# Channel mixers' output projections: 8 of 22 contraction tiles by 7 block products, weight sums by accumulating DMAs

## The chip, the cores and the metric

The kernel runs on one core of a Trainium2 chip. The metric is the device time of one execution, in microseconds; the median of the runs of a kernel is compared with that of the other. Engines are named as in the profile: PE multiplies matrices (PEld loads its stationary operand), DVE and ACT work on tiles elementwise, POOL is the general engine, SP issues DMAs. A bank is one of eight accumulators of 128 x 512 float32 that PE writes.

## The reference, cut to what matters

Two layers, each a token mixer and then a channel mixer, over 512 tokens of width 1024. The change concerns the last product of the channel mixer (2816 = 22 x 128 hidden channels) and the residual behind it.

```python
def conv_ffn(x, w_in, conv_w, conv_b, w_out):
    h = causal_dwconv(x @ w_in, conv_w, conv_b)
    g, u = jnp.split(h, 2, axis=-1)
    return (jax.nn.silu(g) * u) @ w_out
...
        f = conv_ffn(x, ffn_w_in[i], ffn_conv_w[i], ffn_conv_b[i], ffn_w_out[i])
        x = layer_norm(DN_ALPHA * x + f, ln_g[i, 1], ln_b[i, 1])
```

## The kernel before, in words

Every float32 operand is split in two: `hi` is the value rounded to float32r (a cast on ACT), `lo` the rest (a subtraction on DVE). A product is then three matmuls, hi by hi, hi by lo and lo by hi, each 128 x 128 by 128 x 512.

**Weights.** All weights lie in one list `wall` of tiles of 128 x 1024 (512 KB). `w_prep` loads them in list order on SP's queue into `wraw` (3 buffers) and splits them into `whi` and `wlo` (7 buffers each). `w_get(i)` keeps the preparation 6 tiles ahead of use.

**Channel mixer (`ffn`).** The input projection takes 44 weight tiles; each is 8 contraction steps x 3 = 24 matmuls into one bank (`InProj.get`, `mm_k`, lines 126 to 128, moving operands `xT_hi` and `xT_lo`). ACT and DVE apply the convolution and the gate and write `h`, 22 tiles of 128 channels x 512 tokens. The output projection (`out_proj`) then holds all eight banks (`acc`, 4 token tiles x 2 halves of the width) and goes through the 22 contraction tiles: for each, `split.get(k)` splits tile k of `h` into `ahi` and `alo` (6 buffers, lines 192 and 193), and 24 matmuls (lines 214 to 216) add its product to the eight banks. `stats` reads the banks with the residual `xres` (line 259) for the normalisation.

**Order.** The program is built with a tile framework that places instructions on each engine's queue by its own estimate of when they can run; each engine then works strictly through its queue, waiting on semaphores. So what stands ahead of what in a queue is fixed before the run.

Of the kernel before, what the change touches and what calls it, by code (L numbers as in the profile page):

```python
# [47 lines left out]
HEAD = 96  # L48
WB = 7
LOOK = 6  # L50


@with_exitstack
def trunk_kernel(ctx, tc, x_tok, x_t, w_dt, wall, pp, ln_g, ln_b, b_v, b_s, w_s_t, out):
# [15 lines left out]

    wready = {}
    wnext = [0]

    def w_prep(upto):
        while wnext[0] <= min(upto, W_ALL - 1):
            i = wnext[0]
            raw = wpool.tile([P, 1024], F32, tag="wraw", bufs=3, name=f"wraw{i}")
            nc.sync.dma_start(raw, wall[i])
            hi = wpool.tile([P, 1024], F32R, tag="whi", bufs=WB, name=f"whi{i}")
            nc.scalar.copy(hi, raw)  # L80
            lo = wpool.tile([P, 1024], F32R, tag="wlo", bufs=WB, name=f"wlo{i}")
# [41 lines left out]
    def mm_k(o, w, k, lo, hi):  # L123
        whi, wlo = w
        cs = slice(k * P, (k + 1) * P)
        nc.tensor.matmul(o, whi[:, cs], xT_hi[:, k, lo:hi], start=(k == 0), stop=False)  # L126
        nc.tensor.matmul(o, whi[:, cs], xT_lo[:, k, lo:hi], start=False, stop=False)  # L127
        nc.tensor.matmul(o, wlo[:, cs], xT_hi[:, k, lo:hi], start=False, stop=(k == NK - 1))  # L128

    with tc.tile_pool(name="xload", bufs=8) as xl:  # L130
        wdt = xl.tile([P, NK, 32], F32, name="wdt", bufs=1)
        xr = []
        for q in range(4):
            for k in (2 * q, 2 * q + 1):
# [48 lines left out]
    class Split:  # L183
# [3 lines left out]

        def pre(self, k, tag=""):
            bufs = self.bufs if not tag else 1
            hi = self.pl.tile([P, T], F32R, tag="ahi" + tag, bufs=bufs, name=f"ahi{self.base}_{k}")  # L190
            lo = self.pl.tile([P, T], F32R, tag="alo" + tag, bufs=bufs, name=f"alo{self.base}_{k}")
            nc.scalar.copy(hi, self.act(k))  # L192
            nc.vector.tensor_sub(lo, self.act(k), hi.bitcast(F32))  # L193
            self.done[k] = (hi, lo)

        def get(self, k):
# [8 lines left out]
    def out_proj(lnp, split, base, nk, ln, last, hooks=None, nxt=None, mid=None):  # L205
        if last:
            gb, bb = ln_bc(lnp, base, ln)
        acc = [[pst(f"acc{base}_{t}_{h}") for h in range(2)] for t in range(NT)]

        def mm(t, h, k, a, w):  # L210
            o = acc[t][h]
            ts_ = slice(t * P, (t + 1) * P)
            hs = slice(h * T, (h + 1) * T)
            nc.tensor.matmul(o, a[0][:, ts_], w[0][:, hs], start=(k == 0), stop=False)  # L214
            nc.tensor.matmul(o, a[0][:, ts_], w[1][:, hs], start=False, stop=False)  # L215
            nc.tensor.matmul(o, a[1][:, ts_], w[0][:, hs], start=False, stop=(k == nk - 1))  # L216

        k0 = 0
        if hooks is not None:
            k0 = 3  # L220
            aw = []
            for k in range(k0):
                aw.append((split.get(k), w_get(base + k, LOOK - k)))
                for t in range(NT - 1):
                    for h in range(2):
                        mm(t, h, k, *aw[k])
                hooks[0]() if k == 0 else None
            hooks[1]()
            for k in range(k0):
                for h in range(2):  # L230
                    mm(NT - 1, h, k, *aw[k])
# [18 lines left out]
                mm(t, h, k, *aw[k - nm])  # L250

        def stats(t):
            r = lnp.tile([P, D], F32, tag="r", bufs=2, name=f"r{base}_{t}")
            st = block(lnp, 12, f"st{base}_{t}", "st", 2).rearrange("p (a b) -> p a b", a=2)
            mv = block(lnp, 2, f"mv{base}_{t}", "mv", 2)
            rs = block(lnp, 2, f"rs{base}_{t}", "rs", 2)
            for h in range(2):
                hs = slice(h * T, (h + 1) * T)
                nc.vector.scalar_tensor_tensor(r[:, hs], xres[:, t, hs], ALPHA, acc[t][h], ALU.mult, ALU.add)
                nc.vector.bn_stats(st[:, h, :], r[:, hs])  # L260
            nc.vector.bn_aggr(mv, st)
            rstd_of(mv[:, 1:2], rs)
            for h in range(2):
                hs = slice(h * T, (h + 1) * T)
                if last:
                    nc.vector.scalar_tensor_tensor(
                        r[:, hs], r[:, hs], mv[:, 0:1], gb[:, hs], ALU.subtract, ALU.mult)
                    nc.vector.scalar_tensor_tensor(
                        r[:, hs], r[:, hs], rs[:, 1:2], bb[:, hs], ALU.mult, ALU.add)
                    nc.sync.dma_start(out[t * P:(t + 1) * P, hs], r[:, hs])  # L270
                else:
                    nc.vector.tensor_scalar(
                        xres[:, t, hs], r[:, hs], mv[:, 0:1], rs[:, 1:2], ALU.subtract, ALU.mult)

        def trans(t):
            for h in range(2):
                pt = pst(f"pt{base}_{t}_{h}")
                for q in range(4):
                    nc.tensor.transpose(  # L279
                        pt[:, q * P:(q + 1) * P], xres[:, t, h * T + q * P:h * T + (q + 1) * P], ident)  # L280
                xf = lnp.tile([P, 4, P], F32, tag="xf", bufs=2, name=f"xf{base}_{t}_{h}")
                for q in range(4):
                    c = C_LN + ln * 16 + 4 * h + q
                    nc.scalar.activation(  # L284
                        xf[:, q, :], pt[:, q * P:(q + 1) * P], AF.Identity, scale=col(c), bias=col(c + 8))
                xh = xT_hi[:, 4 * h:4 * h + 4, t * P:(t + 1) * P]
                nc.scalar.copy(xh, xf)
                nc.vector.tensor_sub(xT_lo[:, 4 * h:4 * h + 4, t * P:(t + 1) * P], xf, xh.bitcast(F32))

        for t in range(NT):  # L290
            tail(t)
# [5 lines left out]
            nxt(trans)  # L297

    def ln_bc(pl, base, ln):
        gb = pl.tile([P, D], F32, name=f"lng{base}")  # L300
        bb = pl.tile([P, D], F32, name=f"lnb{base}")
# [242 lines left out]
    def ffn(ip, base_o, li, ln, last, nxt=None):  # L544
        with ExitStack() as st:
            hp = pool(st, f"hp{li}")
            h = hp.tile([P, 22, T], F32, name=f"h{li}")
            sp = pool(st, f"sp{li}")
            split = Split(sp, base_o, lambda k: h[:, k, :])
            with ExitStack() as st2:  # L550
                fp = pool(st2, f"fp{li}")
                for j in range(22):
# [2 lines left out]
                    c = C_F + li * 176 + j * 8  # L555
                    pg, pu = ip.get(2 * j), ip.get(2 * j + 1)
                    if j == 1:
                        affine_res(fp, f"f{li}", ln - 1)
                    if j == 21:
                        for kk in range(2):  # L560
                            split.pre(kk)
# [5 lines left out]
            out_proj(lnp, split, base_o, 22, ln, last, nxt=nxt)  # L567


    def v_tile(cb, t, ws):  # L570
        ps = pst(f"pv{cb}_{t}")
        ts_ = slice(t * P, (t + 1) * P)
        for k in range(NK):
            whi = ws[k // 2][0][:, (k % 2) * T:(k % 2) * T + T]
            wlo = ws[k // 2][1][:, (k % 2) * T:(k % 2) * T + T]
            nc.tensor.matmul(ps, xT_hi[:, k, ts_], whi, start=(k == 0), stop=False)  # L576
            nc.tensor.matmul(ps, xT_hi[:, k, ts_], wlo, start=False, stop=False)  # L577
            nc.tensor.matmul(ps, xT_lo[:, k, ts_], whi, start=False, stop=(k == NK - 1))  # L578
        return ps

    v_ready = {}
# [95 lines left out]
def _pack(i):  # L677
# [25 lines left out]
    tiles += [cm(sg[:, :2048]), f("sg_w_out")[0].reshape(16, P, D)]  # L703
    tiles += ffn(1)
    wall = np.concatenate(tiles, 0)

    pp = np.zeros((P, C_ALL), np.float32)
    cw, cb = f("ssm_conv_w")[0], f("ssm_conv_b")[0]
# [52 lines left out]
```

## Time and profile before

| | |
|---|---|
| median of 3 runs | 1440.46 us (1439.75 to 1440.65) |
| profiled execution, its own time | 1439.39 us |
| its span from first to last instruction | 1437.5 us |
| mean granted TensorE clock | 0.999 |
| PE busy | 1423.6 us, 99% of the span |
| DVE busy, ACT busy | 846.1 us (59%), 611.5 us (43%) |
| POOL busy | 23.7 us (2%) |

The profiled execution is 1.07 us below the median, and 1.9 us of it lie outside the span. A busy PE is one with a matmul in flight; matmuls overlap, so the distance from one start to the next tells more than the duration of one.

### The profile page before, as it was taken

The numbers are of one execution on the slowest core, as the hardware profiler recorded it, in microseconds if no ns is written. First come the engines' busy times: TensorE is split into PE (matmuls) and PEld (weight loads), VectorE is DVE, ScalarE is ACT, GpSimd is POOL, SyncE is SP. The second block draws the span as 40 slices with busy tenths as digits, with TensorE's granted clock in tenths as the row PEclk, the third lists the DMA queues.
The fourth block names the chain that finished last, engine by engine and source line by source line (L and its number), as shares of the span: only waits on it lengthen the run. The fifth ranks groups of instructions, "written<-read, shape, count | busy, mean of one in ns | idle before, by whom it ended". The sixth has DMA issues, their size and how long they took to land.

```text
span 1437.5 us, 17317 instructions
## 1 busy us (share of the span) xinstructions
PE 1423.6 (99%) x6911; PEld 1187.8 (83%) x6911; DVE 846.1 (59%) x1147; ACT 611.5 (43%) x893; POOL 23.7 (2%) x30
## 2 busy tenths in 40 slices
PE   8999999999999999999999999999999999999997
PEld 6788888888889888888888888888888888888886
DVE  6878777565378655554336556446378655554336
ACT  5886677343245433333233433223255433333220
POOL 0000000000000000000000000000000000000001
PEclk9999999999999999999999999999999999999999
DMA  6533322333424332323331432223223333333311
GB/s 219 206 106 129 106 100 74 88 115 122 160 73 123 112 99 92 103 90 101 93 98 59 154 125 88 88 88 118 89 81 127 101 103 93 98 103 118 103 44 59
DMA packets 42864, 152.66 MB, mean 106 GB/s; under 512 B 4760, under 2 KB 6040, under 8 KB 41504
## 3 DMA queue, kind: packets, MB, share of 16 engines
q1 hardware_dynamic: 40240, 143.17, 31.0%
q10 hardware_dynamic: 2544, 8.39, 1.7%
q8 instruction: 54, 0.88, 0.2%
q14 instruction: 26, 0.21, 0.0%
HBM read 149.37 MB, written 2.18 MB: 105 GB/s over the span
## 4 chain that ended last, share of the span: by engine, by line
PE 96%; ACT 1%; DVE 1%; DMA 1%; issue 0%; SPq 0%; DVEq 0%; ACTq 0%
PE ip L126 18%; PE ip L127 18%; PE ip L128 18%; PE acc L216 10%; PE acc L214 10%; PE acc L215 10%; PE pv L576 2%; PE pv L578 2%; PE pv L577 2%; PE psp L636 1%; PE py L443 1%; PE pt L279 1%; PE po L450 1%; PE pst L429 1%; PE pcb L384 0%; PE px L395 0%
## 5 line engine op out<-in xcount | busy, mean ns | idle before, releaser
L126 PE MATMUL ip<-xT_hi,whi 128*128 128x512 f32 (+1 forms) x1264 | 484.4, 383 | 0.0
L128 PE MATMUL ip<-xT_hi,wlo 128*128 128x512 f32 (+1 forms) x1264 | 479.8, 380 | 0.0
L127 PE MATMUL ip<-xT_lo,whi 128*128 128x512 f32 (+1 forms) x1264 | 478.7, 379 | 0.0
L82 DVE TENSOR_TENSOR wlo<-wraw,whi 128x1024 fp32r<-128x1024 f32 x242 | 295.7, 1223 | 297.8 <-ACT whi L80 297.3
L80 ACT CAST whi<-wraw 128x1024 fp32r<-128x1024 f32 x242 | 253.8, 1051 | 355.8 <-PE ip L127 289.3
L126 PEld LDWEIGHTS ip<-xT_hi,whi 128*128 128x128 f32 x1264 | 237.9, 188 | 45.3 <-issue 1.2
L128 PEld LDWEIGHTS ip<-xT_hi,wlo 128*128 128x128 f32 x1264 | 237.7, 188 | 44.6
L127 PEld LDWEIGHTS ip<-xT_lo,whi 128*128 128x128 f32 x1264 | 238.0, 188 | 43.3 <-issue 0.2
L214 PE MATMUL acc<-whi,ahi 128*128 128x512 f32 x608 | 237.3, 390 | 0.0
L216 PE MATMUL acc<-whi,alo 128*128 128x512 f32 x608 | 236.6, 389 | 0.0
L215 PE MATMUL acc<-wlo,ahi 128*128 128x512 f32 x608 | 236.5, 389 | 0.0
L214 PEld LDWEIGHTS acc<-whi,ahi 128*128 128x128 f32 x608 | 114.1, 188 | 24.2 <-issue 0.8
L216 PEld LDWEIGHTS acc<-whi,alo 128*128 128x128 f32 x608 | 114.1, 188 | 23.7
L215 PEld LDWEIGHTS acc<-wlo,ahi 128*128 128x128 f32 x608 | 114.1, 188 | 23.6
L193 DVE TENSOR_TENSOR alo<-h,ahi 128x512 fp32r<-128x512 f32 x44 | 30.4, 691 | 103.4 <-ACT ahi L192 103.4
L192 ACT CAST ahi<-h 128x512 fp32r<-128x512 f32 x44 | 27.4, 623 | 141.7 <-PE acc L215 119.5
L180 DVE SCALAR_TENSOR_TENSOR cv<-ip,ppt,cv 128x511 f32<-128x511 f32 (+2 forms) x90 | 66.9, 744 | 2.0 <-ACT cv L178 1.9
L180 DVE SCALAR_TENSOR_TENSOR gt<-ip,ppt,gt 128x511 f32<-128x511 f32 x88 | 65.7, 746 | 1.6 <-ACT gt L178 0.3
L180 DVE SCALAR_TENSOR_TENSOR ut<-ip,ppt,ut 128x511 f32<-128x511 f32 x88 | 65.7, 746 | 1.3
L563 ACT ACTIVATE gt<-gt 128x512 f32<-128x512 f32 x44 | 27.8, 632 | 82.6 <-DVE gt L180 82.5
L284 ACT ACTIVATE xf<-pt,ppt 128x128 f32<-128x128 f32 x96 | 36.6, 466 | 46.0 <-PE pt L279 43.6
L576 PE MATMUL pv<-whi,xT_hi 128*128 128x512 f32 x128 | 50.0, 390 | 0.0
(138 smaller groups left out, 1073.9 us busy)
## 6 DMA issues: line engine op xcount, KB each, us to landing
wraw<-in_wall_dram SPq DMA_DIRECT2D x242, 512.0 KB
xres<-scr SPq DMA_DIRECT2D x8, 1024.0 KB
xr<-in_x_t_dram SPq DMA_DIRECT2D x8, 256.0 KB
xres<-rscr SPq DMA_DIRECT2D x2, 1024.0 KB
xres<-in_x_tok_dram ACTq DMA_DIRECT2D x1, 2048.0 KB
out_dram<-r SPq DMA_DIRECT2D x8, 256.0 KB
wraw_s<-in_wall_dram SPq DMA_DIRECT2D x8, 128.0 KB
lngf<-in_ln_g_dram ACTq DMA_DIRECT2D x2, 512.0 KB
```

The costliest lines, as they stand in the source:

```text
L80: nc.scalar.copy(hi, raw)
L82: nc.vector.tensor_sub(lo, raw, hi.bitcast(F32))
L126: nc.tensor.matmul(o, whi[:, cs], xT_hi[:, k, lo:hi], start=(k == 0), stop=False)
L127: nc.tensor.matmul(o, whi[:, cs], xT_lo[:, k, lo:hi], start=False, stop=False)
L128: nc.tensor.matmul(o, wlo[:, cs], xT_hi[:, k, lo:hi], start=False, stop=(k == NK - 1))
L180: nc.vector.scalar_tensor_tensor(o[:, s:], ps[:, :T - s], col(c + taps - 1 - s), o[:, s:], ALU.mult, ALU.add)
L193: nc.vector.tensor_sub(lo, self.act(k), hi.bitcast(F32))
L214: nc.tensor.matmul(o, a[0][:, ts_], w[0][:, hs], start=(k == 0), stop=False)
L215: nc.tensor.matmul(o, a[0][:, ts_], w[1][:, hs], start=False, stop=False)
L216: nc.tensor.matmul(o, a[1][:, ts_], w[0][:, hs], start=False, stop=(k == nk - 1))
L284: nc.scalar.activation(xf[:, q, :], pt[:, q * P:(q + 1) * P], AF.Identity, scale=col(c), bias=col(c + 8))
L576: nc.tensor.matmul(ps, xT_hi[:, k, ts_], whi, start=(k == 0), stop=False)
```

## The change

The first 8 contraction tiles (tokens 512 x channels 1024, times weights 1024 x 1024) are treated as a 2 x 2 by 2 x 2 block product. A11 to A22 are quarters of `h` (first digit: half of the tokens, second: half of the channels), B11 to B22 quarters of the weights, which lie in `wall` already cut into them (two tiles each, in the order 11, 22, 21, 12). Seven products of 24 matmuls each replace eight tiles of 24:

A11·B11, S4·B22, A12·B21, S1·T1, S2·T2, S3·T3, A22·T4, with S1 = A21 - A22, S2 = A11 - S1, S3 = A21 - A11, S4 = A12 - S2 and T1 = B11 + B12, T2 = T1 + B22, T3 = B22 + B12, T4 = T2 + B21.

The sums S are made on DVE (`sums_first` at step 10 of the input projection, `sums_then` in `seven`). The sums T are made by DMAs: for each half s = 0, 1, SP loads B11 into x and B22 into y, then DMAs from POOL's queue add B12 to x and to y (T1, T3), later B22 to x (T2), later B21 to x (T4). x and y lie in the room of `xT_lo`, which the last matmul of the input projection reads last. Some products go to several quarters of the output: DVE adds them into `xres` from the bank (L291, L298, L302, L306). The program has 6192 rows on PE where it had 6240.

```diff
+    wseq = []
+    for i in range(W_ALL):
+        b = next((b for b in SEVEN if b <= i < b + 8), None)
+        if b is None or i < b + 6:
+            wseq.append(i)
+        elif i == b + 6:
+            wseq += [(b, n, s) for n in ("T1", "T2", "T3", "T4") for s in range(2)]
...
+    def w_sum(b, n, s):
+        def part(q, m):
+            return wall[b + 2 * QUARTER.index(q) + m]
+
+        def more(o, q):
+            nc.gpsimd.dma_start(o, part(q, s), accum_op=ALU.add)
+
+        if n == "T1" and s == 0:
+            c_new(b)
+        x, y = (v[:, 2 * s:2 * s + 2, :].rearrange("p a b -> p (a b)") for v in (craw[0][:, 0:4, :], craw[0][:, 4:8, :]))
+        if n == "T1":
+            nc.sync.dma_start(x, part("11", s))
+            nc.sync.dma_start(y, part("22", s))
+            more(x, "12")
+            more(y, "12")
+        elif n != "T3":
+            more(x, {"T2": "22", "T4": "21"}[n])
+        return y if n == "T3" else x
...
+        def seven():
...
+            prod(qa, *operands("A11", base, base + 1), True)
+            for i in range(2):
+                for m, h, op in ((0, 1, ALU.subtract), (1, 0, ALU.add), (1, 1, ALU.subtract)):
+                    v = xres[:, 2 * m + i, h * T:(h + 1) * T]
+                    nc.vector.scalar_tensor_tensor(v, v, ALPHA, qa[i], ALU.mult, op)
+            prod(qc, *operands("S4", base + 2, base + 3), True)
+            sums()
+            prod(qa, *operands("A12", base + 4, base + 5), False)
+            prod(qb, *operands("S1", *two("T1")), True)
+            for i in range(2):
+                v = xres[:, 2 + i, 0:T]
+                nc.vector.tensor_add(v, v, qb[i])
+            prod(qb, *operands("S2", *two("T2")), False)
...
+            prod(qb, *operands("S3", *two("T3")), False)
...
+            prod(qd, *operands("A22", *two("T4")), True)
...
+        if sums is not None:
+            seven()
+            k0 = 8
```

On DVE's queue, before, the middle of the first channel mixer's output projection alternated between the split of a weight tile and that of an activation tile (the number after a name's letters is the weight tile, 108 being the projection's first; the last number is an instance):

```order
L82 TENSOR_TENSOR wlo117_5338<-wraw117_5334,whi117_5336 128x1024
L193 TENSOR_TENSOR alo108_9_5535<-h0_3719,ahi108_9_5534 128x512
L82 TENSOR_TENSOR wlo118_5372<-wraw118_5368,whi118_5370 128x1024
L193 TENSOR_TENSOR alo108_10_5569<-h0_3719,ahi108_10_5568 128x512
L82 TENSOR_TENSOR wlo119_5406<-wraw119_5402,whi119_5404 128x1024
```

Now the same queue has, from the split of T1's first half on (T2_0 is half 0 of T2; cr holds x and y; acc108_2_1 is the bank of S1·T1, S2·T2 and S3·T3 for the first tokens, acc108_3_1 for the next):

```order
L116 TENSOR_TENSOR wlo108_T1_0_5252<-cr108_5245,whi108_T1_0_5250 128x1024
L241 TENSOR_TENSOR alo108_S2_0_5427<-S2_0_5329,ahi108_S2_0_5426 128x512
L116 TENSOR_TENSOR wlo108_T1_1_5290<-cr108_5245,whi108_T1_1_5288 128x1024
L241 TENSOR_TENSOR alo108_S2_1_5431<-S2_0_5329,ahi108_S2_1_5430 128x512
L116 TENSOR_TENSOR wlo108_T2_0_5295<-cr108_5245,whi108_T2_0_5293 128x1024
L241 TENSOR_TENSOR alo108_S3_0_5473<-h0_3722,ahi108_S3_0_5472 128x512
L116 TENSOR_TENSOR wlo108_T2_1_5334<-cr108_5245,whi108_T2_1_5332 128x1024
L116 TENSOR_TENSOR wlo108_T3_0_5338<-cr108_5245,whi108_T3_0_5336 128x1024
L116 TENSOR_TENSOR wlo108_T3_1_5374<-cr108_5245,whi108_T3_1_5372 128x1024
L116 TENSOR_TENSOR wlo108_T4_0_5379<-cr108_5245,whi108_T4_0_5377 128x1024
L298 TENSOR_TENSOR xres_72<-xres_72,acc108_2_1_5242 128x512
L298 TENSOR_TENSOR xres_72<-xres_72,acc108_3_1_5244 128x512
```

The first read of S1·T1's bank (L298) stands behind the split of T4's first half. In the second channel mixer the splits of T and the two L298 stand in the same order.

On PE's queue, before, the place where the fourth contraction tile hands over to the fifth reads:

```order
L214 MATMUL acc108_0_0_5228<-whi112_5149,ahi108_4_5364 128x512
L215 MATMUL acc108_0_0_5228<-wlo112_5151,ahi108_4_5364 128x512
L216 MATMUL acc108_0_0_5228<-whi112_5149,alo108_4_5365 128x512
L214 MATMUL acc108_0_1_5229<-whi112_5149,ahi108_4_5364 128x512
L215 MATMUL acc108_0_1_5229<-wlo112_5151,ahi108_4_5364 128x512
```

Now, where S1·T1 ends and S2·T2 begins, the queue reads (with what a row waits for):

```order
L273 MATMUL acc108_3_1_5244<-whi108_T1_1_5288,ahi108_S1_1_5385 128x512
L274 MATMUL acc108_3_1_5244<-wlo108_T1_1_5290,ahi108_S1_1_5385 128x512
L275 MATMUL acc108_3_1_5244<-whi108_T1_1_5288,alo108_S1_1_5386 128x512
L273 MATMUL acc108_2_0_5241<-whi108_T4_0_5377,ahi108_A22_0_5518 128x512 [waits Activation_49]
L274 MATMUL acc108_2_0_5241<-wlo108_T4_0_5379,ahi108_A22_0_5518 128x512 [waits DVE_49]
L273 MATMUL acc108_2_1_5242<-whi108_T2_0_5293,ahi108_S2_0_5426 128x512 [waits DVE_49]
```

The first two matmuls of the last product, A22·T4, stand ahead of S2·T2, in both channel mixers.

On POOL's queue nothing stood between one normalisation and the next. Now it has the eight adding DMAs of a mixer, in the order x0, y0, x1, y1 (T1, T3), x0, x1 (T2), x0, x1 (T4); DMAHW is a landing on SP's queue, DMASW one on POOL's:

```order
L89 DMA cr_5245<-in_wall_dram 128x1024 [waits DMAHW6_49,DVE_49,PE_49]
L89 DMA cr_5245<-in_wall_dram 128x1024 [waits DMAHW7_49]
L89 DMA cr_5245<-in_wall_dram 128x1024 [waits DMAHW0_49]
L89 DMA cr_5245<-in_wall_dram 128x1024 [waits DMAHW1_49]
L89 DMA cr_5245<-in_wall_dram 128x1024 [waits DMASW0_49,DVE_49]
L89 DMA cr_5245<-in_wall_dram 128x1024 [waits DMASW2_49,DVE_49]
L89 DMA cr_5245<-in_wall_dram 128x1024 [waits DMASW4_49,DVE_49]
L89 DMA cr_5245<-in_wall_dram 128x1024 [waits DMASW5_49,DVE_49]
```

Each of the last four waits for the landing of the add before it on the same half and for the split that reads that sum.

## Rows read from the trace of the kernel before

**Rows 1.** Page: busy us, share of span, count; then the ending chain by engine
```profile
PE 1423.6 (99%) x6911; PEld 1187.8 (83%) x6911; DVE 846.1 (59%) x1147; ACT 611.5 (43%) x893; POOL 23.7 (2%) x30
...
PE 96%; ACT 1%; DVE 1%; DMA 1%; issue 0%; SPq 0%; DVEq 0%; ACTq 0%
```

**Rows 2.** Busy time by stretch: input, output projection of mixer 1, mixer 2
```profile
core 0: us, PE busy (x) PEld busy (x) DVE busy (x) ACT busy (x) POOL busy (x), PEclk, DMA share, GB/s
440.00:660.00 220.00, 220.00 (x1002) 183.46 (x1001) 135.72 (x160) 88.80 (x111) 0.00 (x0) 1.00 0.32 101
660.00:775.00 115.00, 115.00 (x513) 95.32 (x512) 45.38 (x53) 31.45 (x41) 0.54 (x1) 1.00 0.29 92
1100.00:1310.00 210.00, 210.00 (x928) 173.88 (x927) 123.03 (x146) 83.42 (x103) 0.00 (x0) 1.00 0.34 108
1314.00:1430.00 116.00, 115.98 (x512) 95.72 (x510) 48.13 (x64) 24.22 (x31) 2.87 (x3) 1.00 0.25 81
```

**Rows 3.** Matmuls of line 214 into the banks, mixer 1: ns min/median/max, first, last start
```profile
L214 PE MATMUL acc<-whi,ahi x176: 389/389/481, 665.1 to 785.9; 128*128 128x512 f32 x176
```

**Rows 4.** Timeline of ACT in the output projection: start, us, idle before and releaser
```profile
675.96 0.62 ACT L192 CAST ahi<-h 128x512 fp32r<-128x512 f32 x1 [3.87 <-PE acc L215]
...
681.40 0.62 ACT L192 CAST ahi<-h 128x512 fp32r<-128x512 f32 x1 [3.87 <-PE acc L215]
```

**Rows 5.** Groups by line, 660 to 775 us: busy us, mean ns, idle before, releaser
```profile
L82 DVE TENSOR_TENSOR wlo<-wraw,whi 128x1024 fp32r<-128x1024 f32 x20 | 24.5, 1226 | 17.1 <-ACT whi L80 17.1
L80 ACT CAST whi<-wraw 128x1024 fp32r<-128x1024 f32 x20 | 21.0, 1048 | 13.1 <-PE acc L216 8.5 <-PE ip L127 4.7
L193 DVE TENSOR_TENSOR alo<-h,ahi 128x512 fp32r<-128x512 f32 x16 | 11.1, 692 | 50.6 <-ACT ahi L192 50.6
```

**Rows 6.** Chain that ended last, 24 to 38 us: start, us, what
```profile
28.57 3.63 DMA wraw<-in_wall_dram
...
32.28 1.06 ACT whi L80
...
33.36 1.22 DVE wlo L82
```

**Rows 7.** Busy time by stretch at the start, columns as in Rows 2
```profile
8.00:11.00 3.00, 2.88 (x6) 2.05 (x7) 2.82 (x6) 2.72 (x7) 0.00 (x0) 1.00 1.06 384
14.00:17.00 3.00, 3.00 (x15) 2.49 (x14) 0.89 (x2) 1.01 (x3) 0.00 (x0) 1.00 1.02 390
```

**Rows 8.** Chain that ended last, 0 to 16 us
```profile
8.12 0.80 PE ps_b L126
...
12.63 0.43 PE ps_b L126
13.06 0.41 PE ps_b L127
13.47 0.23 PE ps_b L128
```

**Rows 9.** Waits, 0 to 20 us: who for whom, us in total, times, longest
```profile
PE ps_b L126 <- ACT whi_s L111: 4.7, 1, 4.7
```

**Rows 10.** Waits of SP's queue, 640 to 780 us
```profile
SPq L78 <- DVE wlo L82: 121.0, 24, 5.6
```

**Rows 11.** DVE reading a bank with the residual, mixer 1 (columns as Rows 3)
```profile
L259 DVE SCALAR_TENSOR_TENSOR r<-xres,acc x8: 679/684/689, 765.9 to 787.0; 128x512 f32<-128x512 f32 x8
```

More of the change, by code (lines that the diff above doesn't have):

```diff
@@ L208, in out_proj @@
         acc = [[pst(f"acc{base}_{t}_{h}") for h in range(2)] for t in range(NT)]
+        more = sums is not None
         def mm(t, h, k, a, w):
@@ new lines, in mm, with prod @@
+            nc.tensor.matmul(o, a[1][:, ts_], w[0][:, hs], start=False, stop=(k == nk - 1), skip_group_check=more)
+        def prod(o, a, w, first):
+            for i in range(2):
+                for k in range(4):
+                    ah, al = (v[:, (k % 2) * 256 + i * P:(k % 2) * 256 + (i + 1) * P] for v in a[k // 2])
+                    wh, wl = (v[:, (k % 2) * T:(k % 2) * T + T] for v in w[k // 2])
+                    nc.tensor.matmul(o[i], ah, wh, start=(first and k == 0), stop=False, skip_group_check=True)
+                    nc.tensor.matmul(o[i], ah, wl, start=False, stop=False, skip_group_check=True)
+                    nc.tensor.matmul(o[i], al, wh, start=False, stop=(k == 3), skip_group_check=True)
@@ new lines, in seven, with operands, two @@
+        def seven():
+            qa, qc, qd, qb = ([acc[2 * m][h], acc[2 * m + 1][h]] for m in range(2) for h in range(2))
+            def operands(n, *ws):
+                w = [w_get(x, LOOK - m) for m, x in enumerate(ws)]
+                return [split.get((n, m)) for m in range(2)], w
+            def two(n):
+                return [(base, n, s) for s in range(2)]
+            prod(qa, *operands("A11", base, base + 1), True)
[7 more added lines that the diff above has]
+            prod(qb, *operands("S1", *two("T1")), True)
+            for i in range(2):
+                v = xres[:, 2 + i, 0:T]
+                nc.vector.tensor_add(v, v, qb[i])
+            prod(qb, *operands("S2", *two("T2")), False)
+            for i in range(2):
+                v = xres[:, i, T:]
+                nc.vector.tensor_add(v, v, qb[i])
+            prod(qb, *operands("S3", *two("T3")), False)
+            for i in range(2):
+                v = xres[:, 2 + i, 0:T]
+                nc.vector.tensor_sub(v, v, qb[i])
+            prod(qd, *operands("A22", *two("T4")), True)
+            if not last:
+                x_new(base)
@@ L258, in stats @@
                 hs = slice(h * T, (h + 1) * T)
-                nc.vector.scalar_tensor_tensor(r[:, hs], xres[:, t, hs], ALPHA, acc[t][h], ALU.mult, ALU.add)
+                if sums is not None and (t > 1 or h):
+                    nc.vector.tensor_add(r[:, hs], xres[:, t, hs], acc[t][h])
+                else:
+                    nc.vector.scalar_tensor_tensor(r[:, hs], xres[:, t, hs], ALPHA, acc[t][h], ALU.mult, ALU.add)
                 nc.vector.bn_stats(st[:, h, :], r[:, hs])
@@ L548, in ffn, with quarter, act, tsum @@
             sp = pool(st, f"sp{li}")
-            split = Split(sp, base_o, lambda k: h[:, k, :])
+            tmp = {}
+            def quarter(n):
+                r, c = (4 * (int(v) - 1) for v in n)
+                return h[:, c:c + 4, 64 * r:64 * r + 256]
+            def act(k):
+                if not isinstance(k, tuple):
+                    return h[:, k, :]
+                n, m = k
+                v = tmp[n] if n in tmp else quarter(n[1:])
+                return v[:, 2 * m:2 * m + 2, :]
+            def tsum(n, tag):
+                tmp[n] = sp.tile([P, D], F32, tag=tag, bufs=1, name=f"{n}_{li}").rearrange("p (k t) -> p k t", k=4)
+                return tmp[n]
+            def less(o, a, b):
+                nc.vector.tensor_sub(o, a, b)
+            def sums_first():
+                less(tsum("S1", "lng"), quarter("21"), quarter("22"))
+                less(tsum("S4", "lnb"), quarter("11"), tmp["S1"])
+                less(tmp["S4"], quarter("12"), tmp["S4"])
+                tmp["S3"] = quarter("21")
+                less(tmp["S3"], quarter("21"), quarter("11"))
+            def sums_then():
+                less(tsum("S2", "lnb"), quarter("11"), tmp["S1"])
+            split = Split(sp, base_o, act)
             with ExitStack() as st2:
```

98 lines of the change are left out of this document (63 added, 35 removed).

## The prediction

> **What bounds the kernel now.** I read the page's busy shares and its chain first: PE has a matmul in flight 99% of the span, and 96% of the chain that ended last is PE [rows 1]. Then the stretches: in both input projections and both output projections PE is busy throughout, while DVE is busy 62% (135.72 of 220) and 39% (45.38 of 115), ACT less, the DMA engines 25 to 34%, POOL next to nothing [rows 2]. So only matmuls that go away, or a wait put on PE, can move the time. The matmul's own price is not its 389 ns [rows 3], since they overlap, but the distance of starts: ACT's casts of successive activation tiles, each released by PE, lie 681.40 - 675.96 = 5.44 us apart [rows 4], and 24 matmuls lie between them: 0.227 us each. In this stage SP's loads wait for DVE to free a buffer, 121 us in 24 waits [rows 10]: transfers run ahead of their use.
>
> **What is removed.** 8 tiles of 24 matmuls become 7 products of 24, in two mixers: 48 matmuls (PE's queue has 48 rows less), 48 x 0.227 = 10.9 us. Operands and shapes of the rest are as before, so I price them as before.
>
> **What is added on DVE and ACT.** Five subtractions of 128 x 1024 a mixer (S1, S4 twice, S3, S2), priced as wlo, 1.23 us [rows 5]: 6.1 us. They are issued in the input projection from step 8 on, where DVE is idle 38% of the time [rows 2], and PE has six prepared tiles ahead, 6 x 5.44 = 33 us of cover: nothing. Twelve passes over a bank with xres, 0.68 us each [rows 11], replace nothing: 8.2 us inside the seven products (38.1 us). With the splits due there (12 weight halves at 1.23, 11 activation halves at 0.69 [rows 5]) and about 3 us of convolution left over, DVE has 33.5 us of work in 38.1: enough room by itself, but little, and its queue is strict. Without the cover of the idle time all of it would be 14 us a mixer.
>
> **What is added as a wait.** Call t0 the end of the input projection: x and y lie in `xT_lo`, so nothing can be loaded before t0. S2·T2 is due four products after t0, 21.76 us. But the queues as built put two things in front of it: on PE the first two matmuls of A22·T4, due at 21.76, and on DVE the split of T4's first half ahead of L298, which must empty the bank before S2·T2 writes it (due 22.2 with those two matmuls). So S2·T2 waits not for T2 but for T4, the last link of a serial chain: load B11, add B12, split, add B22, split, add B21, split, then L298. Behind it all of PE waits.
>
> The links that have rows: a 512 KB load took 3.63 us [rows 6]; at 384 to 390 GB/s [rows 7] its data take 0.524 MB / 0.39 = 1.35, so 2.3 are latency. A split is 1.05 on ACT and 1.22 on DVE, one right behind the other [rows 6]: 2.3. L298 0.68. The link that has none is the add. From below: a plain load, 1.35 of data. A gain against a plain load is excluded, since the same bytes come from memory and the buffer must be read besides. From above: reading source and buffer one after the other, 2.7 of data, with the same latency. POOL's own work to issue it is in no row; I leave it at nothing, since it can only lengthen the chain.
>
> Four loads and four adds start together and share the engines, so I let them be served in order: landing = max(issue + 2.3, landing before) + data. The loads land at 3.65, 5.0, 6.35 and 7.7 after t0.
>
> With an add of 1.35: T1's adds x0, y0, x1, y1 land at 9.05, 10.4, 11.75, 13.1. T1_0 is split at 11.35; T2_0 lands at max(11.35 + 2.3, 13.1) + 1.35 = 15.0, split 17.3; T4_0 lands 17.3 + 2.3 + 1.35 = 20.95. T2_1 (after x1, split 14.05) lands 17.7, cast 18.75, and four subtractions stand in DVE's queue from there, T2_1, T3_0, T3_1, T4_0: 18.75 + 4 x 1.22 = 23.6. With L298 24.3: 2.1 us late, 4.2 in both mixers.
>
> With an add of 2.7: 10.4, 13.1, 15.8, 18.5; T1_0 split 12.7; T2_0 max(15.0, 18.5) + 2.7 = 21.2, split 23.5; T4_0 23.5 + 2.3 + 2.7 = 28.5 (T2_1 lands at 23.9, before it), split 30.8, L298 31.5: 9.3 us late, 18.6 in both. After that the next wait, the second half of S3 behind T4_1's split in DVE's queue, is ready at about 35.4 and due at 31.5 + 5.44 + 1.36 = 38.3: covered.
>
> I take 2.7: an add moves twice the bytes of a load through the same engines, and the only rows on those engines at work without a pause, 384 and 390 GB/s at a DMA share of 1.0 [rows 7], show them full with a plain load.
>
> A pause of 9.3 us on PE has a price behind it. At the kernel's start PE waited 4.7 us [rows 9], and then its matmuls came 0.43 us apart until 13.47 and 0.23 after [rows 8]: from 8.12 on, 5.35 us x (1 - 0.227/0.43) = 2.5 us lost, though the granted clock of 8 to 11 reads 1.00 [rows 7]. No row has such a pause inside the kernel: 0 to 2.5 for each. I take 2.5, the pause being twice as long as the one that has a row: 5.0.
>
> The Trainium skill (TensorE: Matmul & The Clock Gate, Part 1) has PE fall from 2.4 to 1.2 GHz when it was idle and recover when it was busy for a while. By it the 5.0 would be due; by the granted clock of 1.00 at the start they would be nothing.
>
> **Sum**, against the profiled execution's own time: 1439.39 - 10.9 + 18.6 + 5.0 = 1452.1. That run is 1.07 below the median of the runs shown, so 1453 beside 1440.46: slower by 0.9%.
>
> **Rivals.**
> 1. *The add costs no more than a load* (faster). For it: the engines are used to 29% in this stage [rows 2], and their read and write sides may overlap. Against it: rows 7. 1439.39 - 10.9 + 4.2 = 1432.7, with the median's 1.07 1434. The change pays as long as L298 is late by less than 5.4 us a mixer and PE does not slow down; that is an add with about 2.0 of data.
> 2. *The chain is hidden altogether* (faster): T4 is split by 21.5. By the rows it takes a link of add and latency under about 3.5, when a plain load is 3.63; then 1428.5 + 1.1 = 1430. The Trainium skill (DMA: Bandwidth & Descriptors, Anatomy of one DMA) fits a DMA from POOL's queue as about 2.0 us + bytes / 436 GB/s; an estimate from that page is 3.2 us for 512 KB, which would hide the chain and give this rival's time. The row for a load, 3.63, is already above that, and the page's fit is for copies.
> 3. *The wait just eats the gain* (same): an add of 2.7 that does not queue behind the others. 3.65 + 3 x (5.0 + 2.3) + 0.68 = 26.2, 4.0 late a mixer, 8.0, and up to 2.5 for one slow restart: 1439.39 - 10.9 + 8.0 + 2.5 = 1439, with 1.07 1440.
> 4. *POOL's issue is long as well*: with 1 us in each of three links, and T1's four queued, the forecast's 9.3 becomes 12.3 to 15: 1459 to 1465. No row speaks for or against.
>
> That the change does not do what it says is excluded by PE's queue, which is 48 rows shorter.
>
> **How the numbers follow.** An add at twice a load's data with a queue, 1442 to 1457: 0.41, taken as the likeliest at 1453. Rival 4: 0.12. Rival 3: 0.11. Rival 1: 0.29. Rival 2: 0.07. Within 0.2% (2.9 us) is about what a measurement here cannot tell from no change. Faster 0.36, same 0.11, slower 0.53. The range leaves out rival 2 and the far end of rival 4: 1432 to 1462; the likeliest case alone is 1442 to 1457.
>
> **What the profile after would show.** Right: PE idle in each mixer once, some 22 us into the output projection, in front of line 273 or 274, released by the split of T4_0 or by L298; the last eight DMAs on POOL's queue 5 us or more from issue to the cast that reads them; matmuls 0.43 apart behind the pause. PE's busy time without the slow stretch lower by 11 us. Wrong: adds that land within 4 us of their release; a pause elsewhere, at S1·T1 (T1_1 is due at 17.7 and I have it split at 18.1 in the dear case) or at the ninth tile, whose weights wait for `wraw` buffers behind T4_1's split; or no slow matmuls behind the pause, which takes 5 us off.

## The result, and the profile after

| | before | after |
|---|---|---|
| median of 4 runs | 1440.11 us (1439.12 to 1440.65) | 1457.05 us (1454.73 to 1458.38) |
| ratio, 95% interval | | 1.0117 (1.0099 to 1.0134): slower |
| profiled execution, its span | 1439.39, 1437.5 us | 1458.38, 1456.4 us |
| PE's matmuls | 6911 | 6863 |

The 48 matmuls are gone, and the kernel is 16.9 us longer (the spans 18.9). The page of the changed kernel, to be read against [rows 1]: busy us, share of the span and count; the chain that ended last; POOL's queue.

```profile
PE 1422.1 (98%) x6863; PEld 1183.4 (81%) x6863; DVE 891.0 (61%) x1205; ACT 627.8 (43%) x917; POOL 37.8 (3%) x46
...
q0 software_dynamic: 2304, 8.39, 3.2%
...
PE 90%; DMA 5%; ACT 2%; DVE 2%; issue 1%; SPq 0%; DVEq 0%; ACTq 0%
...
cr<-in_wall_dram POOLq DMA_DIRECT2D x16, 512.0 KB, 7.7
```

PE's share of the last chain fell from 96 to 90%, and DMA's rose from 1 to 5%. Where that is, the waits of PE show (who for whom: us in all, times, longest):

```profile
PE acc L273 <- ACT ahi_A L240: 14.6, 2, 8.5
...
PE acc L273 <- ACT whi_T L114: 2.6, 2, 2.2
...
PE acc L274 <- DVE wlo_T L116: 1.4, 3, 0.8
```

All three are in the seven products: 18.6 us, where the kernel before has no such wait. To count all that was lost there, I take the 60 us from the first matmul of each output projection (t0). Busy time by stretch, columns as in Rows 2, in the kernel before and then in the changed kernel:

```profile
665.11:725.11 60.00, 60.00 (x266) 49.71 (x265) 22.51 (x24) 17.62 (x23) 0.00 (x0) 1.00 0.31 96
1310.14:1370.14 60.00, 60.00 (x266) 49.71 (x265) 22.43 (x24) 17.62 (x23) 0.00 (x0) 1.00 0.37 113
```

```profile
665.38:725.38 60.00, 50.47 (x207) 40.18 (x206) 37.88 (x46) 24.97 (x32) 7.12 (x8) 0.91 0.69 167
1318.49:1378.49 60.00, 50.87 (x196) 39.81 (x195) 36.00 (x44) 23.88 (x32) 6.85 (x8) 0.89 0.74 180
```

PE has 266 matmuls in each of the first two, and 59 and 70 fewer in the others: 129 x 0.227 = 29.3 us lost. With 10.9 saved that is +18.4, and the spans say +18.9, so all but half a microsecond lies there. I call this count "the loss" below. Its course in mixer 1 is in the chain that ended last (start, us, what), where t0 is 665.4:

```profile
669.48 7.95 DMA cr<-in_wall_dram
677.45 1.06 ACT whi_T L114
678.53 1.24 DVE wlo_T L116
679.77 0.29 issue
680.06 7.33 DMA cr<-in_wall_dram
687.41 1.06 ACT whi_T L114
688.50 1.23 DVE wlo_T L116
689.73 0.29 issue
690.02 5.67 DMA cr<-in_wall_dram
695.81 0.91 issue
696.72 0.62 ACT ahi_A L240
697.39 0.79 PE acc L273
698.18 0.74 PE acc L274
698.92 0.60 PE acc L273
699.52 0.43 PE acc L274
...
703.36 0.37 PE acc L274
703.74 0.23 PE acc L275
```

Three adds stand in series, each with cast and subtraction behind it: 7.95, 7.33 and 5.67 us. The third is T4's. PE's two A22 matmuls start (697.39) when T4's cast is done and, right behind it in ACT's queue, that of A22's own activations (`ahi_A`), which the profile names as the releaser. S2's first matmul follows at about 698.7, 33.4 us after t0, and matmuls then start 0.43 us apart until 703.7. From 665 to 682 they were 0.23 apart at a granted clock of 1.00, that is 2.4 GHz; the granted clock of 697 to 704 is 0.53, so most of it ran at the lower level, 1.2 GHz.

### The profile page after: what moved, and what is told of

Its sections match the earlier page's. It is cut to its first block, busy times and chain, and to the rows that moved or that the text cites. A ratio compares the mean times of both kernels' runs of the same rounds, so it can differ in the third digit from the quotient of the medians.

```text
span 1456.4 us, 17352 instructions
## 1 busy us (share of the span) xinstructions
PE 1422.1 (98%) x6863; PEld 1183.4 (81%) x6863; DVE 891.0 (61%) x1205; ACT 627.8 (43%) x917; POOL 37.8 (3%) x46
## 4 chain that ended last, share of the span: by engine, by line
PE 90%; DMA 5%; ACT 2%; DVE 2%; issue 1%; SPq 0%; DVEq 0%; ACTq 0%
PE ip L169 18%; PE ip L171 18%; PE ip L170 18%; PE acc L264 7%; PE acc L265 7%; PE acc L266 7%; DMA cr<-in_wall_dram 3%; PE pv L712 2%; PE pv L710 2%; PE pv L711 2%; PE acc L273 1%; PE acc L274 1%; PE acc L275 1%; PE psp L770 1%; PE py L545 1%; PE pt L381 1%
## 5 line engine op out<-in xcount | busy, mean ns | idle before, releaser
L116 DVE TENSOR_TENSOR wlo<-wraw,whi 128x1024 fp32r<-128x1024 f32 x238 | 290.3, 1221 | 280.8 <-ACT whi L114 280.2
L114 ACT CAST whi<-wraw 128x1024 fp32r<-128x1024 f32 x238 | 249.5, 1051 | 353.8 <-PE ip L170 289.1
L170 PEld LDWEIGHTS ip<-xT_lo,whi 128*128 128x128 f32 x1264 | 238.0, 188 | 43.4 <-issue 0.2
L264 PE MATMUL acc<-whi,ahi 128*128 128x512 f32 x480 | 187.6, 391 | 0.0
L266 PE MATMUL acc<-whi,alo 128*128 128x512 f32 x480 | 186.9, 389 | 0.0
L265 PE MATMUL acc<-wlo,ahi 128*128 128x512 f32 x480 | 186.8, 389 | 0.0
L264 PEld LDWEIGHTS acc<-whi,ahi 128*128 128x128 f32 x480 | 90.1, 188 | 19.3 <-issue 0.8
L266 PEld LDWEIGHTS acc<-whi,alo 128*128 128x128 f32 x480 | 90.1, 188 | 18.8
L265 PEld LDWEIGHTS acc<-wlo,ahi 128*128 128x128 f32 x480 | 90.2, 188 | 18.4
L386 ACT ACTIVATE xf<-pt,ppt 128x128 f32<-128x128 f32 x96 | 36.6, 467 | 45.8 <-PE pt L381 43.7
L241 DVE TENSOR_TENSOR alo<-h,ahi 128x512 fp32r<-128x512 f32 x28 | 19.3, 690 | 53.1 <-ACT ahi L240 53.1
L240 ACT CAST ahi<-h 128x512 fp32r<-128x512 f32 x28 | 17.4, 621 | 77.5 <-PE acc L265 45.9
```

Of the source, the lines that this page charges most:

```text
L170: nc.tensor.matmul(o, whi[:, cs], xT[1][:, k, lo:hi], start=False, stop=False)
L386: nc.scalar.activation(xf[:, q, :], pt[:, q * P:(q + 1) * P], AF.Identity, scale=col(c), bias=col(c + 8))
```

## The experiments

Ratios are to the kernel before, run on the same chip; it took 1439.2 to 1440.1 us there, so medians of two rows compare to within 0.9 us. The loss is counted as above (in warm without the matmuls that the version adds). In the texts TensorE is PE, VectorE DVE, ScalarE ACT and GpSimd POOL. Line numbers shift with each edit: the additions behind S1·T1, L298 in the changed kernel, are also L301, L302, L307 or L309.

| version | median us | ratio (95%) | loss, mixer 1 + 2, us |
|---|---|---|---|
| changed kernel | 1457.05 | 1.0117 (1.0099 to 1.0134) | 13.4 + 15.9 |
| no_adds | 1428.47 | 0.9919 (0.9902 to 0.9936) | 0 + 0 |
| copy_pool | 1442.16 | 1.0021 (1.0011 to 1.0031) | 5.0 + 7.7 |
| warm | 1457.51 | 1.0120 (1.0104 to 1.0136) | 12.7 + 15.0 |
| t4_behind | 1451.64 | 1.0081 (1.0066 to 1.0096) | 10.7 + 12.3 |
| x_first | 1455.88 | 1.0116 (1.0101 to 1.0131) | 11.8 + 14.5 |
| chain_ordered | 1453.98 | 1.0096 (1.0082 to 1.0110) | 13.6 + 12.0 |
| chain_clean | 1446.85 | 1.0051 (1.0038 to 1.0065) | 6.4 + 12.3 |
| pool_add | 1457.67 | 1.0131 (1.0116 to 1.0146) | 15.2 + 13.8 |
| dve_add | 1438.95 | 0.9996 (0.9987 to 1.0006) | 5.0 + 5.2 |
| dve_ordered | 1431.93 | 0.9943 (0.9929 to 0.9956) | 0.9 + 1.1 |
| mixed | 1434.95 | 0.9965 (0.9954 to 0.9975) | 1.8 + 3.9 |
| mixed_clean | 1429.32 | 0.9932 (0.9919 to 0.9946) | 0 + 0.2 |

My theory: the loss is the chain of accumulating transfers ahead of S2·T2, long because an add holds the DMA engines for twice a load's time, and longer because T4 stands ahead of S2 in the queues. Rivals: the additions on VectorE; GpSimd's queue, whatever it carries; the slow matmuls behind the pause.

### Is it the adds?

**no_adds**

```
         def more(o, q):
-            nc.gpsimd.dma_start(o, part(q, s), accum_op=ALU.add)
+            pass
```

> The sixteen accumulating transfers are left out (T1 and T2 and T4 are then just B11, T3 just B22), so the chain of additions is gone and everything else of the change stands. Theory (the loss is the chain of adds and the pause it makes): 1440.1 less 48 matmuls of 0.227 = 10.9, so 1429 (1427 to 1432), and no pause of TensorE before the A22 product. Rival (the loss lies in the sums and extra additions on VectorE and ScalarE, or in the order of the products): 1436 to 1457, with a pause released by VectorE that is not a weight split.

1428.47, and PE has 266 matmuls in both stretches, so not one was lost:

```profile
666.38:726.38 60.00, 60.00 (x266) 49.70 (x265) 41.57 (x50) 28.10 (x37) 0.00 (x0) 1.00 0.38 122
1305.98:1365.98 60.00, 60.00 (x266) 49.70 (x265) 41.65 (x50) 28.00 (x37) 0.00 (x0) 1.00 0.42 140
```

Everything else in the change is hidden; its 10.9 us are real (10.7 measured), and the adds cost 28.6 us. The first rival fell.

**copy_pool**

```
-            nc.gpsimd.dma_start(o, part(q, s), accum_op=ALU.add)
+            nc.gpsimd.dma_start(o, part(q, s))
```

> The sixteen transfers stay on GpSimd's queue with the same waits, but they copy and do not accumulate (the additions of weight blocks are left out). Theory (accumulating is what is dear: 5.6 us for an add alone against 3.63 for a load): each of the three serial steps gets about 1.7 to 4 us shorter, T4's split comes 5 to 9 us earlier, and the time falls to 1438 to 1446. Rival (GpSimd's queue and its issue of 0.85 us are dear, whatever the transfer does): issue to cast stays at 5.6 to 7.7 us and the time at 1453 to 1458.

1442.16, as the theory said: the accumulation alone is 14.9 us. The DMA view of 660 to 705 us (queue: packets, MB, share of 16 engines) has, in the changed kernel,

```profile
q0 software_dynamic: 1152, 4.19, 52.3%
```

and, with the copies,

```profile
q0 software_dynamic: 1152, 4.19, 27.1%
```

The same packets and bytes: 0.523 x 45 / 8 = 2.94 us of all engines for an add, 1.52 for a copy, 1.93 to 1. T4's add, which starts with the DMA engines idle (their share is 0.01 from 690 to 691), takes 5.67 us in the chain above; the copy in its place took (chain that ended last):

```profile
685.06 3.65 DMA cr<-in_wall_dram
```

That is near the 3.63 of SP's load [rows 6], so GpSimd's queue is no dearer by itself. But it issues an add in 0.85 us and a copy in 0.54. GpSimd's timeline in the changed kernel, then with copies (start, us; idle before, releaser):

```profile
690.02 0.85 POOL L89 DMA_DIRECT2D cr<-in_wall_dram  x1 [4.10 <-DVE wlo_T L116]
```

```profile
685.06 0.54 POOL L89 DMA_DIRECT2D cr<-in_wall_dram  x1 [3.23 <-DVE wlo_T L116]
```

The Trainium skill (Collectives: The Full Stack, The bandwidth ceiling: the fold count and why AG ≠ RS ≠ AR) says of ReduceScatter, whose DMAs add, that it is slower than AllGather not for the arithmetic but because each add reads two sources through the same ring, and gives a measured ratio of 1.93 between the two. The 1.93 of this trace agrees in size; that the second read is the reason here too is not shown by a run.

### Is it the slow matmuls?

**warm**

```
-            prod(qb, *operands("S1", *two("T1")), True)
+            z, (_, ah, wh) = prod(qb, *operands("S1", *two("T1")), True)
+            with tc.issue_after(z):
+                for i in range(30):
+                    nc.tensor.matmul(qd[0], ah, wh, start=True, stop=True, skip_group_check=True)
```

> Thirty matmuls more, behind S1's on TensorE's queue, with a result that is thrown away: 6.8 us of work at 0.227 in the pause of 8.5 us (mixer 1) and of 6.2 us (mixer 2). Theory (the slow matmuls behind the pause are a cost of their own, 0.43 apart for some 6 us in each mixer, so about 3 us each): the first matmul of A22 comes when it came, but those behind it are 0.23 apart, and the time falls to 1451 to 1453, though TensorE does more. Rival (those matmuls were late because their data were): 1457 or more, up to 1459 where the thirty last past the split in mixer 2.

1457.51: no change, the rival's time. The timeline of PE in this version, mixer 1 and mixer 2 (start, us; idle before):

```profile
690.28 6.96 PE L299 MATMUL acc<-whi_T,ahi_S 128*128 128x512 f32 x30
700.09 0.47 PE L273 MATMUL acc<-whi_T,ahi_S 128*128 128x512 f32 x1 [2.85 <-DVE xres L302]
...
1347.33 6.96 PE L299 MATMUL acc<-whi_T,ahi_S 128*128 128x512 f32 x30
1355.70 0.47 PE L273 MATMUL acc<-whi_T,ahi_S 128*128 128x512 f32 x1 [1.41 <-DVE xres L302]
```

S2 starts 32.8 and 36.1 us after its t0, against 33.4 and 35.8 in the changed kernel: the data set that, not PE. Behind the 2.85 us pause eight matmuls are still 0.43 apart; behind the 1.41 none is, and the granted clock of 1352 to 1360 is 1.00, where the changed kernel has 0.57. So slow matmuls follow from the pause, as the theory had it, but they are worth little: in the changed kernel the first eleven distances between S2's matmuls took 4.85 and 4.74 us in place of 2.5, 2.3 us a mixer. By the count of the loss the filler saved 1.6 us of that, 27.7 for 29.3. The median does not show it; the profiled execution lost about 2 us far ahead of the filler, at 41 to 44 us, where its matmuls are 0.43 apart behind a pause and those of the changed kernel 0.23. The 4 to 6 us that I expected were not there.

### Is it the order?

**t4_behind**

```
-            prod(qb, *operands("S2", *two("T2")), False)
+            with tc.issue_after(z.ins):
+                s2 = operands("S2", *two("T2"))
+            prod(qb, *s2, False)
...
-            prod(qd, *operands("A22", *two("T4")), True)
+            a22 = operands("A22", *two("T4"))
+            with tc.issue_after(z):
+                prod(qd, *a22, True)
```

Here z is first the last addition of line 298, then the last matmul of S3. S1 prepares one step less ahead, and S2's activation splits stay ahead of the additions.

> All is computed; only the order changes: T4's split and what follows it in the preparation is put behind S1's additions (the two of line 298) on VectorE, and the A22 matmuls behind S3's on TensorE. Theory (the S2 product waits for T4 only because of the queues): S2 now waits for T2 alone, whose splits ended about 24.7 and 27.6 us into the projection where 21.8 and 23.1 were due, so about 4.5 us late per mixer and not 10 to 12, with a shorter slow stretch behind it: 1444 (1440 to 1449). Rival (the length of the chain decides, wherever T4 stands): the pause moves to the A22 product and the time stays above 1452.

1451.64: 5.4 us back, less than half of what I expected, and between the ranges of theory and rival. S2 no longer waits for T4 (its first matmul came 30.7 us after t0, before T4's cast), but VectorE's timeline shows the next thing in its queue:

```profile
691.41 3.50 DVE L116 TENSOR_TENSOR wlo_T<-cr,whi_T 128x1024 fp32r<-128x1024 f32 x3 [1.10 <-ACT whi_T L114]
694.83 0.68 DVE L301 TENSOR_TENSOR xres<-xres,acc 128x512 f32<-128x512 f32 x1
```

Those three are T2's second half, which S2 needs, and both halves of T3, which it does not.

**x_first** has the edit above, prepares less far ahead in A12 and S1 so that T3's splits also come behind S1's additions, and changes the order of the adds:

```
             nc.sync.dma_start(x, part("11", s))
-            nc.sync.dma_start(y, part("22", s))
             more(x, "12")
-            more(y, "12")
-        elif n != "T3":
-            more(x, {"T2": "22", "T4": "21"}[n])
+            if s == 1:
+                for m in range(2):
+                    nc.sync.dma_start(craw[0][:, 4 + 2 * m:6 + 2 * m, :].rearrange("p a b -> p (a b)"), part("22", m))
+        elif n == "T3":
+            with tc.issue_after(last[0]):
+                more(y, "12")
+        else:
+            last[0] = more(x, {"T2": "22", "T4": "21"}[n])
```

> All is computed; the same sixteen accumulating transfers, in another order: both adds of T1, both of T2, then those of T3, then T4's; and the splits of T3 and T4 stand behind S1's additions on VectorE, the A22 matmuls behind S3's on TensorE. Eight adds took 52.3% of 45 us of the queue in the changed kernel, 2.94 us of all engines each, so T1's pair lands about 7 us after the loads, T2's pair about 9 us later with its split: some 22 to 24 us into the projection, where 21.8 is due. Theory (what counts is how many adds stand ahead of T2's split): S2 comes 1 to 3 us late per mixer, 1434 (1429 to 1441). Rival (the chain's length alone decides, T1 then T2 in series, with T3's adds not in the way): as with only T4 put behind, 1448 to 1453.

1455.88, above both ranges, and a trap of my own. VectorE's timeline:

```profile
689.43 1.23 DVE L122 TENSOR_TENSOR wlo_T<-cr,whi_T 128x1024 fp32r<-128x1024 f32 x1 [1.41 <-ACT whi_T L120]
...
691.78 0.68 DVE L307 TENSOR_TENSOR xres<-xres,acc 128x512 f32<-128x512 f32 x1
698.54 0.69 DVE L247 TENSOR_TENSOR alo_A<-h,ahi_A 128x512 fp32r<-128x512 f32 x1 [6.09 <-ACT ahi_A L246]
699.15 0.68 DVE L307 TENSOR_TENSOR xres<-xres,acc 128x512 f32<-128x512 f32 x1
```

T2's split is complete at 690.7, 24.8 us after t0, close to the 22 to 24 expected. But between the two additions that S2 needs, the queue has A22's activation split, whose cast stands behind T4's on ScalarE: 6.1 us for data that A22 alone uses. Neither theory nor rival as I wrote them had this.

**chain_ordered** puts T3's splits behind S1's additions, T4's behind S2's, and A22's activation splits early:

```
             with tc.issue_after(z.ins):
-                s2 = operands("S2", *two("T2"))
+                s2 = operands("S2", *two("T2"), look=3)
+                for m in range(2):
+                    split.pre(("A22", m))
...
+            with tc.issue_after(z2.ins):
+                s3 = operands("S3", *two("T3"))
```

> All sums by accumulating transfers, in the order T1, T2, T3, T4, and every split on VectorE behind the additions of the product before, the A22 matmuls behind S3's. Theory (with no split standing ahead of work that does not need it, what is left is the chain itself): in the run with T2 first its second split was done 24.8 us into the projection and T4's second cast began at 33.6; S2 then 3 to 5 us late, A22 4 to 5 us late in all, and the slow matmuls behind the pause: 1437 to 1446. Rival (one more entry of a queue stands ahead of S2 or S3): 1449 or more.

1453.98, the rival: A22's early splits now stood ahead of S2's additions (L317) and behind T4's casts, and S3 waited 3.9 us in mixer 1. VectorE's timeline:

```profile
701.91 0.69 DVE L247 TENSOR_TENSOR alo_A<-h,ahi_A 128x512 fp32r<-128x512 f32 x1 [1.80 <-ACT ahi_A L246]
702.52 0.68 DVE L317 TENSOR_TENSOR xres<-xres,acc 128x512 f32<-128x512 f32 x1
```

**chain_clean** moves them three lines down, into the second block (z2 is S2's last addition).

> As the ordered chain of accumulating transfers, but A22's own splits are put behind S2's additions: in the run before they stood ahead of them on VectorE and behind T4's first cast on ScalarE, and S3 waited 3.9 us for that. Theory (what now remains is the price of the chain itself): S2 still 4.9 us (mixer 1) and 8 to 9 us (mixer 2) late, S3 about 1 us more, against 5.44 saved in each: 1444 to 1449, so slower than the kernel before even with every entry in place. Rival (the chain costs little, the queue entries were all): 1440 or less.

1446.85, inside the range, with this as the only wait of any length in the seven products (waits of PE):

```profile
PE acc L279 <- DVE xres L309: 13.6, 2, 9.2
```

4.5 and 9.2 us, both in front of S2. With every queue entry in place the chain of two adds still costs more (82 matmuls, 18.6 us) than the products save (10.9). Order, that of the adds among themselves and that of the splits together, was 29.3 - 18.6 = 10.7 us of the loss.

### Sums elsewhere

**pool_add** and **dve_add** make each sum with a tensor addition (on GpSimd, on VectorE), with B12 and B21 loaded into the raw buffers:

```
-            nc.gpsimd.dma_start(o, part(q, s), accum_op=ALU.add)
+            if (q, s) not in rraw:
+                rraw[q, s] = wpool.tile([P, 1024], F32, tag="wraw", bufs=3, name=f"wraw{b}_{q}_{s}")
+                nc.sync.dma_start(rraw[q, s], part(q, s))
+            nc.gpsimd.tensor_add(o, o, rraw[q, s])
```

> All is computed; the sums are made by GpSimd's tensor additions of 128x1024 (eight per mixer) in place of the accumulating transfers, with B12 and B21 loaded into the raw buffers on SyncE's queue, B22 read where it lies. The order of splits and products is left. Not shown by any run so far is the duration of such an addition; VectorE's of the same size takes 1.24 us. Theory (only the transfers' chain is slow): with 1.24 to 3 us for an addition, T4's split is done 3.6 + 3 x (1.24 to 3 + 2.3) = 14 to 19.5 us into the projection, ahead of 21.8: no pause, 1429 (1427 to 1434). Rival (GpSimd's additions take 4.5 us or more, or slow VectorE down): a pause again, 1438 to 1457.

1457.67: the estimate missed. What came was the rival's pause, and of its two conditions the second, VectorE slowed down. An addition takes 2.4 us, inside my range where nothing holds it up, but eight follow each other on one engine, T4's first is the seventh, and the additions and VectorE's subtractions hold each other up. GpSimd's timeline:

```profile
670.93 2.41 POOL L94 TENSOR_TENSOR cr<-cr,wraw 128x1024 f32<-128x1024 f32 x1 [240.61 <-DMA cr<-in_wall_dram]
...
683.09 3.35 POOL L105 TENSOR_TENSOR cr<-cr 128x1024 f32<-128x1024 f32 x1
```

and VectorE's:

```profile
674.45 2.84 DVE L124 TENSOR_TENSOR wlo_T<-cr,whi_T 128x1024 fp32r<-128x1024 f32 x1 [0.57 <-ACT whi_T L122]
...
694.78 2.83 DVE L249 TENSOR_TENSOR alo_S<-h,ahi_S 128x512 fp32r<-128x512 f32 x1
697.53 1.21 DVE L124 TENSOR_TENSOR wlo_T<-cr,whi_T 128x1024 fp32r<-128x1024 f32 x1
```

The subtraction of 1.21 us takes 2.84 beside GpSimd, the one of 0.69 takes 2.83.

> As with GpSimd's additions, but on VectorE: eight more instructions of 1.24 us = 9.9 us per mixer on an engine that has 33.5 us to do in the seven products' 38.1. Theory (VectorE is then the bound of the seven products): up to 5.3 us longer per mixer, 1434 to 1440, with TensorE waiting for VectorE. Rival (a good part of VectorE's work there is ahead of its time): 1428 to 1433.

1438.95, no change against the kernel before, inside the theory's range. But PE's waits were 2.6 us a mixer, for T4's split and for A22's activations behind T4's cast, so it was not settled that VectorE was the bound. **dve_ordered** takes the order of chain_ordered:

> All sums on VectorE as before (eight additions per mixer), but in the order of the products: T3's splits behind S1's additions, T4's sums and splits behind S2's, and the A22 matmuls behind S3's on TensorE. Theory (a part of the 5 us per mixer that the sums on VectorE cost was T4 standing ahead of S2): 1432 to 1436. Rival (VectorE's 43.4 us of work in 38.1 us is the bound whatever the order): 1438 to 1441, as without the order.

1431.93, at the lower end of the theory's range: order again, 7 us of it. VectorE with 43.4 us of work by my count hardly stretched the products: in mixer 1 they took 38.8 us, VectorE was busy 36.6 of these, and the rest of the count lies outside them.

**mixed** makes T1 and T2 on VectorE and leaves T3 and T4 to the transfers, in the order of chain_ordered; **mixed_clean** in that of chain_clean:

```
+            own(x, "12")
+        elif n == "T2":
+            nc.vector.tensor_add(x, x, y)
+        else:
+            more(*((y, "12") if n == "T3" else (x, "21")))
```

Here own loads the block into a raw buffer and adds it on VectorE.

> All is computed. The sums that are due first (T1 and T2, four additions of 128x1024 per mixer) are made on VectorE, with B12 loaded into the raw buffers; T3's and T4's (due later) stay accumulating transfers, four per mixer. Each split stands on VectorE's queue in the order in which the products come: T1, T2, S1's additions, T3, S2's additions, T4, S3's. VectorE gets 4 x 1.24 = 5 us more than its 33.5 in 38.1. Theory (the loss was the serial adds ahead of S2 and the queue order): T2 is split some 18 us into the projection, T3 by about 26 (due 27.2), T4 by about 31 (due 32.6), so little or no pause: 1430 (1428 to 1435), faster than the kernel before. Rival (VectorE is full, and the transfers still late): 1438 or more.

> As the mixed sums (T1 and T2 on VectorE, T3 and T4 by accumulating transfers), with A22's splits behind S2's additions, where they stood ahead of the second of these and S3 waited 1.6 and 2.0 us. Theory (transfers that are off the chain are hidden): those two waits go, 1430 to 1433, as with all sums on VectorE. Rival (T3's transfers, landed 24.5 and 26 us into the projection, are themselves what S3 waited for): 1434 to 1436, no change.

1434.95, at the upper end of its range, then 1429.32, just below its range. In mixed, S3 waited 1.6 and 2.0 us for S2's second addition, behind A22's splits as in chain_ordered; without that the whole gain is there (busy time by stretch, mixed_clean):

```profile
666.83:726.83 60.00, 60.00 (x266) 49.56 (x265) 45.50 (x54) 28.34 (x37) 3.64 (x4) 1.00 0.62 174
1306.51:1366.51 60.00, 59.94 (x265) 49.34 (x264) 45.49 (x54) 28.16 (x36) 3.44 (x4) 1.00 0.67 191
```

One matmul of 129 is still missing. The eight accumulating transfers that are left take 7.2 us from issue to landing (the median; 7.7 in the changed kernel), but T3 and T4 are due late enough. This version beats both kernels: 0.9932 (0.9919 to 0.9946).

## Why the prediction was right, and where it was off

The forecast of a slower kernel, its place and its mechanism held; the time is 4 us beyond it by the medians, and 6.3 by the profiled executions (1458.38 for 1452.1), whose terms are compared here.

- **Removed work, 10.9 us:** right; no_adds gives 10.7, and shows that the additions on DVE and ACT are hidden as said.
- **The add costs twice a load:** right. I took 2.7 us of data from rows of a plain load; it is 2.94, against 1.52 for a copy. Rival 1 needed 1.35 and rival 2 a link under 3.5; the shortest here is 5.63. The Trainium skill's fit for a copy (DMA: Bandwidth & Descriptors, Anatomy of one DMA), 3.2 us by my estimate, is near the 3.65 of a copy and far from an add.
- **S2 waits for T4 through the queues:** right, and t4_behind removes it. That T3's splits stand there as well I had counted in the sum for the cheap add alone; that they would be the next wait I had not seen.
- **The length of the chain, 9.3 us late a mixer:** mis-sized. S2's first matmul, due at 22.2, came 33.4 and 35.8 us after t0: 11.2 and 13.6 late, 24.8 in place of 18.6. In mixer 1 the steps are T1_0's cast at 12.1 (forecast 10.4), T2_0's at 22.0 (21.2), T4_0's at 30.4 (28.5). The term that each link lacks is POOL's issue, which I left at nothing because no row had it: it is 0.85 us. In T4's link, where no other add is in the way, the rest of the transfer takes 4.8 where I had 5.0, so the issue is what was missing. Where four adds share the engines, 2.94 for 2.7 comes on top; the two are not separated there. So a part of rival 4 was true (1 us a link). That the 12.3 us that it began with is near the mean of the two mixers, 12.4, is luck, for 2.5 us of mixer 2's 13.6 do not come from POOL's issue. In mixer 2 T1_0 was cast only at 14.6; the layer norm's two loads of 512 KB were issued on ACT's queue at 1321.9 and 1322.3, just ahead of the first adds (1322.9), and I had not counted them. The DMA view of 1316 to 1360 us has them in a queue of their own, 1.05 MB and 8.8% of the 16 engines: 0.088 x 44 = 3.9 us of all engines, enough for the 2.5 us. And where no transfer adds (dve_add, dve_ordered), the two mixers lose alike. That they are the cause was not tried by a run.
- **Slow restart, 2.5 us a pause:** right in size, 2.3 each by rows of the changed kernel, where the granted clock reads 0.53 and 0.57. The 1.00 beside matmuls 0.43 apart at the start [rows 7, 8] was no evidence against it: the trace of the kernel before has no record of the clock ahead of 13.3 us, and the view prints 1.00 where there is none. The matmuls come 0.23 apart from 13.5 on, where the records begin at full clock.
- **Signs:** PE's pause came where named, in front of L273, though its releaser in the profile is the cast of A22's activations behind T4's cast, which I had not listed; S2's first matmul then came right behind L298, as said. But PE also paused 1.1 and 2.9 us at S1·T1, which I had listed as a sign against: T1_1, forecast 0.4 late, was later.

Together: 1439.39 - 10.9 + 24.8 + 4.6 = 1457.9, the profiled run's 1458.38 within 0.5. Not settled is how much of the loss is each part by itself, since they overlap: without the accumulation 12.7 are left of 29.3, with the order in place 18.6, with the adds left out none.

## What to carry to other kernels

Look at what stands ahead in every in-order queue before shortening a chain: the same sums in a better order went from 1457 to 1447 us, and three of the orders tried here failed on an entry or two that wait for data their successor does not need. A sum made by an accumulating transfer was free here only where it is due late: the fastest version has the first links of the serial chain on an engine with short instructions (1.23 us each on VectorE) and leaves the rest to the DMAs. And price a "free" add in a DMA as two loads plus its issue, as it came out here (2.94 us against 1.52, and 0.85 of issue).

## What the runs showed of the hardware

- An accumulating transfer of 512 KB held the 16 DMA engines for 2.94 us, a copy of the same blocks from the same queue for 1.52; alone 5.67 against 3.65 from issue to landing, of which GpSimd's issue is 0.85 against 0.54.
- A GpSimd addition of 128x1024 takes 2.41 us where it is not held up and up to 3.35 beside VectorE, and VectorE's subtraction of 128x512 takes 2.83 in place of 0.69 beside it. The Trainium skill (SBUF — State Buffer, Who interferes with whom) has the two engines share a port under a lock that one holds for its whole instruction, also where VectorE reads two inputs from SBUF; 2.83 - 0.69 = 2.14, nearly a whole addition, agrees with that.
